# The second gate unit's multiply moved by two steps, and a new order in the tail, in a streaming-encoder block on one core

## The chip, the cores and the metric

The kernel runs on one core of one Trainium2 chip. The time is that of one execution on the device, in microseconds; a kernel's time is the median of its runs. A core has five engines with queues of their own: TensorE (PE), VectorE (DVE), ScalarE (ACT), GpSimd (POOL) and SyncE (SP). SP, ACT and POOL issue DMAs.

## What is computed

One layer over 512 tokens of 2048 features, all in float32, in this form:

```
h = rms_norm(x); q_a,k_a,v_a,q_g,k_g,v_g,r_g,gate_lr = split(h @ w_in)
y_a = chunked_band_attention(q_a, k_a, v_a)            # 16 heads of 64
o_g = rms_norm(gated_linear_attention(q_g, k_g, v_g))  # 4 heads of 256 values
y_g = o_g * silu(r_g)
x = x + concat(y_a, y_g) @ w_out
u = causal_conv3(rms_norm(x) @ w_ffn_up)               # 2 x 5632 columns
x = x + (gelu(u_gate) * u_val) @ w_ffn_down
x = x + sigmoid(rms_norm(x) @ w_ple_gate) * (p @ w_ple_proj)
return rms_norm(x)
```

## The kernel before

**Products.** Activations lie transposed, features on the 128 partitions and tokens along the free axis. A unit is one pair of 128-row blocks of a result (block m and block m + 8, or a gate and a value block). Each unit is computed by seven products in Strassen's manner, named P1 to P7, each over 256 tokens; a product is collected into a quarter of the unit's output tile `u` (C11, C12, C21, C22; the first digit is the block, the second the half of the tokens). Float32 precision comes from three passes with operands that are split into a high and a low half: high weights by high data, high weights by low data, low weights by high data. With 8 blocks of depth a product has 3 x 8 = 24 matmuls of 128 x 256. For each product ACT makes the high half of the weight page (`w<-s` or `w<-l`) and DVE the low half (`w<-s,w`); three page slots go round, so the high half of step i + 2 waits for the product of step i - 1. Some weight pages are sums of others: a load on SP and an adding DMA on POOL, or an addition on DVE (`s<-s,l`).

**Steps and agenda.** `steps` lists every product in order, and `agenda[i]` holds the pieces of side work of step i, each with a key. At step i the main loop runs the pieces with key 0, makes the high half for step i + 2, runs those with key 1, makes that page's low half, issues the product, runs the pieces with keys 2 to 8, and collects the product. PE, DVE and ACT execute in exactly this order (`in_order(True)`). The DMAs on SP and POOL are not held to it: a scheduler places them when the program is built.

**The front stage.** Its units are four of linear attention, eight of attention (`attend`) and four gate units (`after_gates`, u = 8 to 11, so g = 0 to 3), seven steps each. The second gate unit is g = 1: its products are steps 91 to 97, and its side work is counted from step 98, which is the first product of the third gate unit. That side work is: load `on` (the normed output of linear attention, from the DRAM tile `ond`) by SP; Silu of the unit's output on ACT; the multiply `u<-u,on` on DVE (`times`); and `pair`, which calls `store_pair`: three stores of `u` quarters, four differences on DVE into `tp`, and their four stores, all on SP. `after_gates` returns these pieces as tuples (steps later, key, function). For g = 2 the multiply and the pair come two steps later than the load. For g = 0 the whole list comes six steps after the unit's last product (`late`). After the front stage comes a stage of four steps for p @ w_ple_proj (`pp`), then `wo`, the product with w_out.

**The tail.** The last stage is the PLE gate. Its last two units, u6 and u7, end with the order P5, P5, P3, P3 written out by hand behind the main loop. `lo` is the first half of the tokens (0 to 255), `hi` the second. The helpers of the tail:

- `collect(u, "P3")`: DVE adds the product in PSUM to the unit's quarter (`u<-u,accC`).
- `times_norm(u, s, c)`: DVE multiplies a quarter by the norm's factor (`u<-u,rb`), then ACT takes the sigmoid.
- `add_gated(u, s, c)`: DVE multiplies by the embedding term and adds to the residual `xs`, ACT writes the square into `q`.
- `weigh_part`: ACT multiplies a block of `xs` by the final norm's weight.
- `sums_by_token`: PE sums squares over the partitions into `ms`. `root_begin` and `root_end`: ACT takes the square root, DVE refines it and writes two diagonals `dg`. `spread`: PE makes the row of factors `pb` from them.
- `finish(c, r, ms, queue)`: for each block pair m, DVE multiplies by `pb` and a DMA of 256 KB stores it, on SP or on the queue named. `turn` and `turned_out` do it another way for block pairs 0 to 3 of the second half: PE transposes, ACT evicts with the factor as a scale per partition, SP stores. `turn_first` and `turned_first_out` do that for block pair 4 of the first half.
- `act.activation(warm, ..., AF.Sqrt)` brings in the table of Sqrt ahead of its use.

Sixteen stores of 256 KB make the whole output: eight block pairs for each half of the tokens.

Of the kernel before, what the change touches and what calls it, by code (L numbers as in the profile page):

```python
# [11 lines left out]
AF = mybir.ActivationFunctionType  # L12
# [30 lines left out]
def encoder_block(ctx: ExitStack, tc: tile.TileContext, A, out):  # L43
    nc = tc.nc
# [25 lines left out]
    vec, act, ten = InOrder(nc.vector), InOrder(nc.scalar), InOrder(nc.tensor)  # L70
# [10 lines left out]
    ones = cp.tile([P, P], F32, name="ones")  # L81
# [3 lines left out]
    warm = cp.tile([P, 1], F32, name="warm")  # L85
# [3 lines left out]
    acc = cp.tile([P, T], F32, name="acc")  # L89
# [13 lines left out]
    def page(ring, name, dt=F32, shape=(P, 1024)):  # L103
        tags = rings[ring]
        i = counts.get(ring, 0)
        counts[ring] = i + 1
        tag = tags[i % len(tags)]
        return page_pool(tag).tile(list(shape), dt, tag=tag, name=name)
# [11 lines left out]
    def psum_aux(name):  # L120
        return aux[0](name)
# [106 lines left out]
    def xslot(i, name):  # L228
        return pairs[i % 8][:, i // 8, :]
# [7 lines left out]
    first = xslot(0, "x0_0")  # L237
# [307 lines left out]
    def bank(name):  # L545
        tag = banks.pop(0)
        return tag, pp_.tile([P, T], F32, tag=tag, name=name)
# [22 lines left out]
    def collect(unit, prod):  # L570

        if prod == "PP":
            return
        b = PRODUCTS[prod][2]
        tag, t = unit.banks[b]
        t = t[:, 0:256]
        unit.left[b] -= 1
        if unit.left[b] == 0:
            banks.append(tag)
        if unit.o is None:  # L580
            unit.o = page("u", "u").rearrange("p (s t) -> p s t", s=2)
        quarter, sign = {"P1": ("C11", 1), "P2": ("C11", 1), "P6": ("C12", 1), "P5": ("C22", -1),
                         "P7": ("C22", -1), "P3": ("C12", 1), "P4": ("C21", -1)}[prod]
        s, h = int(quarter[1]) - 1, int(quarter[2]) - 1
        dst = unit.o[:, s, 256 * h:256 * h + 256]
        if quarter not in unit.have:
            unit.have.add(quarter)
            act.activation(dst, t, AF.Copy, scale=float(sign))
        else:
            vec.tensor_tensor(dst, dst, t, ALU.add if sign > 0 else ALU.subtract)  # L590
        unit.parts[quarter] -= 1
        if unit.last is not None and unit.stage.quarter and unit.parts[quarter] == 0:
            unit.stage.quarter(unit, quarter)
# [282 lines left out]
    def after_gates(unit):  # L876
        g, M = unit.u - 8, {}

        def load():
            M["on"] = page("x" if g == 0 else "c", "on").rearrange("p (s t) -> p s t", s=2)  # L880
            nc.sync.dma_start(M["on"], ond[g])

        def times():
            vec.tensor_tensor(unit.o, unit.o, M["on"], ALU.mult)

        def pair():
            ops = store_pair(mixd if g < 2 else None, 4 + g, unit.o[:, 0, :], unit.o[:, 1, :])
            if g >= 2:
                tails[g - 2] = ops

        return [(0, 0, load), (0, 1, lambda: act.activation(unit.o, unit.o, AF.Silu)), (2 * (g == 2), 2, times), (2 * (g == 2), 3, pair)]

    def front_weights(u, q):
        j = ({"1": u, "2": 8 + u}[q[1]] if u < 8 else 24 + 2 * (u - 8) + (q[1] == "2") if u < 12 else
# [141 lines left out]
    def spare(name):  # L1036
        tag = free.pop(0)
        return page_pool(tag).tile([P, 1024], F32, tag=tag, name=name)

    def times_norm(unit, s, c):  # L1040
        o = unit.o[:, s, c]
        r = rb[:, None, c].broadcast_to([P, 2, 256]) if isinstance(s, slice) else rb[:, c]
        vec.tensor_tensor(o, o, r, ALU.mult)
        act.activation(o, o, AF.Sigmoid)

    def add_gated(unit, s, c):
        o, xs = unit.o[:, s, c], unit.xs[:, s, c]
        vec.tensor_tensor(o, o, unit.pp[:, s, c], ALU.mult)
        vec.tensor_tensor(xs, xs, o, ALU.add)
        if unit not in sq_page:  # L1050
            sq_page[unit] = spare("q").rearrange("p (s t) -> p s t", s=2)
        act.activation(sq_page[unit][:, s, c], xs, AF.Square)
# [524 lines left out]
    for i, (unit, prod) in enumerate(steps[:-4]):  # L1577
# [24 lines left out]
        if i - len(steps) in EARLY:  # L1602
            p, op, g = EARLY[i - len(steps)]
# [20 lines left out]
    def sums_by_token(parts, ms=None, done=True):  # L1624

        first = ms is None
        if first:
            ms = psum_aux("ms")[:, :2]
        for n, q in enumerate(parts):
            for t in range(2):  # L1630
                ten.matmul(ms[:, t:t + 1], q[:, t * P:t * P + P], ones[:, 0:1], start=first and n == t == 0,
                           stop=done and n == len(parts) - 1, skip_group_check=True)
        return ms

    def root_begin(ms):
        w = tp.tile([P, 4 * TT], F32, tag="tok", name="tok", bufs=2)
        a, y, t, r = (w[:, 2 * q:2 * q + 2] for q in range(4))
        act.activation(y, ms, AF.Sqrt, scale=1.0 / D, bias=epst)
        vec.tensor_scalar(a, ms, 1.0 / D, EPS, ALU.mult, ALU.add)
        return a, y, t, r  # L1640
# [11 lines left out]
    def spread(dg):  # L1652
        pb = bank("pb")[1][:, 0:256]
        ten.matmul(pb, ones, dg, start=True, stop=True)
        return pb

    def finish(c, r, ms, queue=None):
        for m in ms:
            t = x3[m][:, :, c]
            vec.tensor_tensor(t, t, r[:, None, :].broadcast_to([P, 2, 256]), ALU.mult)  # L1660
            (queue or nc.sync).dma_start(out2[m][:, :, c], t)

    u6, u7 = units[-2:]
    x3[6], x3[7] = u6.xs, u7.xs

    def weigh_part(unit, ss, c):
        for s in ss:
            m = unit.u + 8 * s
            act.activation(unit.xs[:, s, c], unit.xs[:, s, c], AF.Copy, scale=nfin[:, m:m + 1])


    def turn(n):
        t = bank("turned")[1]
        for b in range(4):
            m, s = 2 * (n % 2) + b // 2, b % 2
            c = slice(256 + n // 2 * P, 384 + n // 2 * P)
            ten.transpose(t[:, b * P:b * P + P], x3[m][:, s, c], ident)
        return t

    def turned_out(n, t, r):  # L1680
        if n % 2 == 0:
            turned_page[:] = [spare("turned")]
        o = turned_page[0][:, n % 2 * T:n % 2 * T + T]
        act.activation(o, t, AF.Copy, scale=r[:, n // 2:n // 2 + 1])
        m = 2 * (n % 2)
        nc.sync.dma_start(out2[m + n // 2][:, :, hi_half], o.rearrange("p (s t) -> p s t", s=2))
# [4 lines left out]
    def turn_first(m):  # L1691
        t = psum_aux("turned")
        for b in range(4):
            ten.transpose(t[:, b * P:b * P + P], x3[m][:, b % 2, b // 2 * P:b // 2 * P + P], ident)
        return t

    def turned_first_out(m, t, r):
        o = spare("turned")[:, :T]
        for i in range(2):
            c = slice(256 * i, 256 * i + 256)  # L1700
            act.activation(o[:, c], t[:, c], AF.Copy, scale=r[:, i:i + 1])
        nc.sync.dma_start(out2[m][:, :, lo_half], o.rearrange("p (s t) -> p s t", s=2))


    lo, hi = lo_half, hi_half
    sq = lambda u, s, c: sq_page[u][:, s, c]
    ms, rs = {}, {}
# [14 lines left out]
    w0 = root_begin(ms["lo"])  # L1722
# [6 lines left out]
    times_norm(u6, 0, hi)  # L1729
    weigh_part(u7, range(2), lo)  # L1730
    finish(lo, rs["lo"], (0,))
    add_gated(u6, 0, hi)
    weigh_part(u7, (1,), hi)
    weigh_part(u6, (1, 0), hi)
    finish(lo, rs["lo"], (1,))
    collect(u7, "P3")
    m1 = sums_by_token([acc[:, hi], sq(u6, 1, hi), sq(u7, 1, hi)], done=False)
    turned = [turn(n) for n in range(2)]
    m1 = sums_by_token([sq(u6, 0, hi)], m1, done=False)
    turned += [turn(n) for n in range(2, 4)]  # L1740
    first = turn_first(4)
    times_norm(u7, 0, hi)
    act.activation(warm, ones[:, 0:1], AF.Sqrt)
    finish(lo, rs["lo"], (2,))
    add_gated(u7, 0, hi)
    m1 = sums_by_token([sq(u7, 0, hi)], m1)
    finish(lo, rs["lo"], (3, 6))
    turned_first_out(4, first, w0[3])
    w1 = root_begin(m1)
    d1 = root_end(hi, *w1)  # L1750
    rs["hi"] = spread(d1)
    finish(lo, rs["lo"], (7,))
    turned_out(0, turned[0], w1[3])
    finish(hi, rs["hi"], (4,))
    turned_out(1, turned[1], w1[3])
    weigh_part(u7, (0,), hi)
    finish(hi, rs["hi"], (5,))
    turned_out(2, turned[2], w1[3])
    finish(hi, rs["hi"], (6,), nc.scalar)
    turned_out(3, turned[3], w1[3])  # L1760
    finish(hi, rs["hi"], (7,))
    finish(lo, rs["lo"], (5,), nc.scalar)


def _blocks(w):
# [73 lines left out]
```

## Time and profile before

| | |
|---|---|
| median of 3 runs | 2208.3 us (2207.74 to 2209.05) |
| profiled execution | 2206.61 us |
| its span on the core | 2204.7 us |
| granted TensorE clock, mean | 0.998 |
| PE busy | 2179.5 us (99%) |
| DVE busy | 1891.3 us (86%) |
| ACT busy | 1320.9 us (60%) |
| DMA traffic | 569.77 MB, mean 258 GB/s |

The span is the part of the execution in which the core's engines work; the profiled execution is 1.9 us longer. PE is busy for nearly all of the span, so the time moves where PE waits, at the start, at a few places within, and in the tail after its last product. All numbers of the trace come from this one execution, and times in it are counted from the start of the span. Lines are mostly given as L64, the helper through which ordered instructions pass, so instructions are told apart by engine and tiles, output first: `u<-u,on` reads tiles `u` and `on` and writes `u`.

### The profile page before, as it was taken

What the parts mean: (1) busy time and instruction counts of PE and PEld (TensorE: products, weight loads), DVE (VectorE), ACT (ScalarE), POOL (GpSimd) and SP (SyncE); (2) the same over time, 40 slices, a digit from 0 to 9 for tenths busy, and PEclk for the clock granted to TensorE, in tenths of its full rate; (3) what the DMA queues carried; (4) which work ended last, traced back from release to release, by engine and by line L of the source; (5) the groups of instructions that cost most, each with busy time, mean ns of one, the idle gap of its engine ahead of it and who ended that gap; (6) DMA issues with size and microseconds to landing.
All of it is one profiled execution on the core that took longest, in us unless ns stands there. A gap on an engine that the chain in (4) does not pass through costs nothing.

```text
span 2204.7 us, 45658 instructions
## 1 busy us (share of the span) xinstructions
PE 2179.5 (99%) x18248; PEld 2128.6 (97%) x18248; DVE 1891.3 (86%) x2601; ACT 1320.9 (60%) x1960; POOL 201.3 (9%) x245
## 2 busy tenths in 40 slices
PE   9999999999999999999999999999999999999997
PEld 7879999999899999999999999999999999999997
DVE  6876879998688889999888888889898797898997
ACT  6654567777575665555555555555564554666765
POOL 1021011111000001111111110000000100000000
PEclk9999999999999999999999999999999999999999
DMA  5498798898978989999999987887866967879896
GB/s 205 134 268 238 206 245 239 216 249 242 366 259 269 345 234 267 296 298 300 289 273 293 271 241 212 227 220 211 254 240 232 324 223 240 324 256 349 276 303 204
DMA packets 202341, 569.77 MB, mean 258 GB/s; under 512 B 22065, under 2 KB 64305, under 8 KB 202129
## 3 DMA queue, kind: packets, MB, share of 16 engines
q1 hardware_dynamic: 167792, 448.06, 57.3%
q0 software_dynamic: 32352, 115.88, 27.6%
q8 instruction: 143, 2.34, 0.4%
q10 hardware_dynamic: 1984, 2.92, 0.4%
q14 instruction: 70, 0.57, 0.1%
HBM read 493.37 MB, written 119.54 MB: 278 GB/s over the span
## 4 chain that ended last, share of the span: by engine, by line
PE 82%; DVE 8%; DMA 5%; ACT 2%; issue 2%; POOL 0%; DVEq 0%; SPq 0%; ACTq 0%; POOLq 0%
PE accA L64 41%; PE accC L64 20%; PE accB L64 10%; PE v L64 4%; DVE w L64 3%; PE vaA L64 2%; DVE h L64 1%; PE pp L64 1%; DVE u L64 1%; DMA on<-ond 1%; DMA s<-in_w_blk 1%; DMA s<-in_w_up 1%; DMA h<-h_T 1%; PE psc L64 1%; PE py L64 1%
## 5 line engine op out<-in xcount | busy, mean ns | idle before, releaser
L64 PE MATMUL accA<-h,w 128*128 128x256 f32 x5088 | 613.1, 277 | 2.5 <-ACT u L64 1.5
L64 PEld LDWEIGHTS accA<-h,w 128*128 128x128 f32 x5088 | 594.2, 188 | 5.6 <-ACT u L64 2.3
L64 DVE TENSOR_TENSOR w<-s,w 128x1024 fp32r<-128x1024 f32 (+1 forms) x381 | 457.5, 1201 | 68.4 <-ACT w L64 67.5
L64 PE MATMUL accC<-h,w 128*128 128x256 f32 x4248 | 509.9, 277 | 2.7 <-DVE w L64 2.7
L64 PEld LDWEIGHTS accC<-h,w 128*128 128x128 f32 x4248 | 494.4, 188 | 3.4 <-DVE w L64 3.1
L64 ACT ACTIVATE w<-l 128x1024 fp32r<-128x1024 f32 (+1 forms) x320 | 332.0, 1039 | 178.3 <-PE accC L64 116.9
L64 DVE TENSOR_TENSOR w<-l,w 128x1024 fp32r<-128x1024 f32 (+1 forms) x320 | 382.6, 1196 | 51.4 <-ACT w L64 49.2
L64 ACT ACTIVATE w<-s 128x1024 fp32r<-128x1024 f32 (+1 forms) x381 | 395.0, 1038 | 41.6 <-DVE s L64 28.7
L64 ACT ACTIVATE u<-accA 128x256 f32<-128x256 f32 x302 | 114.1, 378 | 349.0 <-PE accA L64 348.6
L64 DVE TENSOR_TENSOR s<-s,l 128x1024 f32<-128x1024 f32 (+1 forms) x176 | 211.3, 1201 | 18.1 <-DMA s<-in_w_blk 11.1
L64 POOL DMA_DIRECT2D s<-in_w_up x84 | 74.0, 881 | 716.3 <-DMA s<-in_w_up 335.8
L64 DVE SCALAR_TENSOR_TENSOR cv<-u,cw,cv 128x511 f32<-128x511 f32 (+1 forms) x176 | 131.6, 748 | 3.1
L64 PE MATMUL accA<-up_R,w 128*128 128x256 f32 x1056 | 127.0, 276 | 0.0
L64 PE MATMUL accA<-up_N,w 128*128 128x256 f32 x1056 | 126.7, 276 | 0.1
L64 PE MATMUL accB<-up_R,w 128*128 128x256 f32 x1056 | 126.7, 276 | 0.0
L64 PEld LDWEIGHTS accA<-up_R,w 128*128 128x128 f32 x1056 | 123.0, 188 | 0.5 <-issue 0.5
L64 PEld LDWEIGHTS accA<-up_N,w 128*128 128x128 f32 x1056 | 122.9, 188 | 0.3 <-ACT u L64 0.3
L64 PEld LDWEIGHTS accB<-up_R,w 128*128 128x128 f32 x1056 | 123.0, 188 | 0.0
L64 ACT ACTIVATE u<-accC 128x256 f32<-128x256 f32 x98 | 37.4, 381 | 91.0 <-PE accC L64 90.8
L64 PE MATMUL v<-w,h 128*128 128x512 f32 x384 | 88.7, 391 | 0.8 <-ACT h L171 0.8
L64 PEld LDWEIGHTS v<-w,h 128*128 128x128 f32 x384 | 71.9, 188 | 16.5 <-ACT h L171 1.0
L64 ACT ACTIVATE cv<-u,cw 128x512 f32<-128x512 f32 x88 | 67.1, 810 | 30.4 <-DVE u L64 30.4
(302 smaller groups left out, 2851.2 us busy)
## 6 DMA issues: line engine op xcount, KB each, us to landing
l<-in_w_up SPq DMA_DIRECT2D x132, 512.0 KB, 6.5
s<-in_w_up SPq DMA_DIRECT2D x84, 512.0 KB, 6.3
s<-in_w_up POOLq DMA_DIRECT2D x84, 512.0 KB, 7.9
l<-in_w_dn SPq DMA_DIRECT2D x56, 448.0 KB, 5.0
l<-in_w_blk SPq DMA_DIRECT2D x48, 512.0 KB, 5.2
s<-in_w_blk SPq DMA_DIRECT2D x32, 512.0 KB, 4.9
s<-in_w_blk POOLq DMA_DIRECT2D x32, 512.0 KB, 8.2
l<-in_w_out SPq DMA_DIRECT2D x28, 512.0 KB, 4.5
```

What stands on the lines that cost most here:

```text
L64: ins = f(*args, **kw)
```

## The change

It has two parts.

In `after_gates` the condition `g == 2` becomes `g in (1, 2)`: the second gate unit's `times` and `pair` run at step 100 in place of 98, with the same keys, behind the product of that step. Load and Silu stay at step 98.

In the tail, after the first output multiply of the first half, the order is written anew. The collection of u7's last product and its norm multiply come directly there. The three weightings of the second half that stood there go behind the beginning of the root. The sums of u6's last square come together with those of u7. All four transposed tiles and the fifth come in a row. The output multiplies of the first half are 1, 2, 3 ahead of the root and 6, 7, 5 behind it, where they were 1, 2, 3, 6 ahead, 7 behind and 5 at the very end. The turned block pair 4 is evicted behind the root's square root. The eviction of the last turned tile comes ahead of the store of block pair 6, and the store of block pair 7 of the second half goes to ACT's queue, which held that of block pair 5 of the first half. No instruction is added or dropped.

```
-        return [(0, 0, load), (0, 1, lambda: act.activation(unit.o, unit.o, AF.Silu)), (2 * (g == 2), 2, times), (2 * (g == 2), 3, pair)]
+        return [(0, 0, load), (0, 1, lambda: act.activation(unit.o, unit.o, AF.Silu)), (2 * (g in (1, 2)), 2, times), (2 * (g in (1, 2)), 3, pair)]
...
     finish(lo, rs["lo"], (0,))
+    collect(u7, "P3")
+    times_norm(u7, 0, hi)
     add_gated(u6, 0, hi)
+    act.activation(warm, ones[:, 0:1], AF.Sqrt)
+    m1 = sums_by_token([acc[:, hi], sq(u6, 1, hi), sq(u7, 1, hi)], done=False)
+    turned = [turn(n) for n in range(4)]
+    first = turn_first(4)
+    add_gated(u7, 0, hi)
+    m1 = sums_by_token([sq(u6, 0, hi), sq(u7, 0, hi)], m1)
+    finish(lo, rs["lo"], (1, 2, 3))
+    w1 = root_begin(m1)
+    turned_first_out(4, first, w0[3])
     weigh_part(u7, (1,), hi)
     weigh_part(u6, (1, 0), hi)
-    finish(lo, rs["lo"], (1,))
-    collect(u7, "P3")
-    m1 = sums_by_token([acc[:, hi], sq(u6, 1, hi), sq(u7, 1, hi)], done=False)
-    turned = [turn(n) for n in range(2)]
-    m1 = sums_by_token([sq(u6, 0, hi)], m1, done=False)
-    turned += [turn(n) for n in range(2, 4)]
-    first = turn_first(4)
-    times_norm(u7, 0, hi)
-    act.activation(warm, ones[:, 0:1], AF.Sqrt)
-    finish(lo, rs["lo"], (2,))
-    add_gated(u7, 0, hi)
-    m1 = sums_by_token([sq(u7, 0, hi)], m1)
-    finish(lo, rs["lo"], (3, 6))
-    turned_first_out(4, first, w0[3])
-    w1 = root_begin(m1)
     d1 = root_end(hi, *w1)
     rs["hi"] = spread(d1)
-    finish(lo, rs["lo"], (7,))
+    finish(lo, rs["lo"], (6, 7, 5))
     turned_out(0, turned[0], w1[3])
     finish(hi, rs["hi"], (4,))
     turned_out(1, turned[1], w1[3])
     weigh_part(u7, (0,), hi)
     finish(hi, rs["hi"], (5,))
     turned_out(2, turned[2], w1[3])
+    turned_out(3, turned[3], w1[3])
     finish(hi, rs["hi"], (6,), nc.scalar)
-    turned_out(3, turned[3], w1[3])
-    finish(hi, rs["hi"], (7,))
-    finish(lo, rs["lo"], (5,), nc.scalar)
+    finish(hi, rs["hi"], (7,), nc.scalar)
```

## The prediction, made before the run

> **What bounds the kernel now.** I began with the page, to see which engine holds the span.
>
> ```profile
> span 2204.7 us, 45658 instructions
> ...
> PE 2179.5 (99%) x18248; PEld 2128.6 (97%) x18248; DVE 1891.3 (86%) x2601; ACT 1320.9 (60%) x1960; POOL 201.3 (9%) x245
> ```
>
> TensorE (PE) is busy for all but about 25 us of the span, so a change can only win where PE stands idle, and only two such places touch this change. The first is around 550 us, at the end of the front stage. There I read the chain of waits, in order of time:
>
> ```profile
> 545.11 9.33 DMA on<-ond
> ...
> 554.53 1.24 DVE u L64
> ...
> 555.79 1.11 DVE tp L64 x3
> ...
> 557.26 1.23 DVE w L64
> ...
> 558.53 1.19 PE accC L64 x8
> ```
>
> Read it downwards. The load of the second gate unit's `on` runs for 9.33 us, from 545.11 to 554.44. Only then does VectorE (DVE) run that unit's multiply (`u`, 1.24 us), then its pair of differences (`tp`), and only then, at 557.26, the low half of a weight page (`w`), for which PE waits until 558.53. The waits of 535 to 600 us put lengths to it:
>
> ```profile
> DVE u L64 <- DMA on<-ond: 3.7, 1, 3.7
> ...
> PE accC L64 <- DVE w L64: 2.5, 1, 2.5
> ```
>
> DVE stands still for 3.7 us with everything queued behind the multiply, and 2.5 us of that reach PE. That is the whole price of the place; there is no other PE wait in this stretch.
>
> The second place is the tail, after PE's last product near 2187 us, where a chain over ScalarE (ACT), DVE and PE leads through the last root to the output multiplies and their stores. Its rows stand below, where they are priced.
>
> **Part one: the second gate unit's multiply, two steps back.** No instruction is added or removed. The multiply, the four differences of its pair, and the seven stores that the pair issues move from step 98 to step 100 (a step is one product of 24 matmuls). What DVE is now free to do first is seen in the timeline; columns are start, length, engine, operation, and in brackets the idle time before it:
>
> ```profile
> 549.12 1.05 ACT L64 ACTIVATE w<-s 128x1024 fp32r<-128x1024 f32 x1
> ...
> 549.58 1.22 DVE L64 TENSOR_TENSOR w<-s,w 128x1024 fp32r<-128x1024 f32 x1
> ...
> 550.65 1.06 ACT L64 ACTIVATE w<-s 128x1024 fp32r<-128x1024 f32 x1 [0.48 <-PE accB L64]
> ...
> 551.36 2.88 PE L64 MATMUL accA<-h,w 128*128 128x256 f32 x24
> ...
> 554.08 1.98 PE L64 MATMUL accC<-h,w 128*128 128x256 f32 x16
> ...
> 558.39 0.41 DVE L64 TENSOR_TENSOR u<-u,accB 128x256 f32<-128x256 f32 x1
> ...
> 558.72 1.22 DVE L64 TENSOR_TENSOR s<-s,l 128x1024 f32<-128x1024 f32 x1
> ...
> 560.04 1.07 ACT L64 ACTIVATE w<-s 128x1024 fp32r<-128x1024 f32 x1 [5.37 <-DVE s L64]
> ```
>
> PE's steps are 2.72 us apart (551.36 to 554.08). Step 101 is the product at 554.08: 16 matmuls ran with the high half, then PE stopped for the low half. That low half needs only the high half made by ACT at 549.12 (done 550.17), and DVE is through with the previous low half at 550.80 (549.58 + 1.22). So in the new order DVE does it at 550.8, done about 552.0; PE's third pass of step 101 wants it at 554.08 + 1.81 (two thirds of 2.72) = 555.9. The wait is gone with 3.9 us to spare. Then follow the collection of step 99 (0.41), the sum page `s` (1.22) and the low half of step 102, whose high half ACT has ready at 550.65 + 1.06 = 551.71: 552.0 + 0.4 + 1.2 + 1.2 gives 554.8. There the multiply now stands, and its data landed at 554.44, so by these rows it waits for nothing. Multiply and differences take until 557.26 − 554.53 = 2.7 us later, 557.5. Behind them is queued the low half of step 103, then done at 558.7. Step 103 starts at 554.08 + 2 × 2.72 = 559.5 and wants it at 561.3. ACT's high half for that step, which now waits 5.4 us for the sum page, comes earlier too. So the moved work is covered by DVE's own slack, and if the load landed later than 554.8, 2.6 us of further lateness (561.3 − 558.7) would still cost PE nothing.
>
> The gain is thus 2.5 us, unless something else is late next. The stores' absolute time hardly moves (the multiply runs at 554.8 against 554.53), so the queues of SP and POOL see them where they were. But PE comes 2.5 us earlier to what follows, while loads do not. The nearest margin is the third gate unit:
>
> ```profile
> 565.57 0.61 SPq L881 DMA_DIRECT2D on<-ond  x1
> ...
> 575.96 1.22 DVE L64 TENSOR_TENSOR u<-u,on 128x1024 f32<-128x1024 f32 x1
> ...
> 578.60 2.88 PE L64 MATMUL accA<-h,w 128*128 128x256 f32 x24
> ...
> 578.69 1.22 DVE L64 TENSOR_TENSOR w<-s,w 128x1024 fp32r<-128x1024 f32 x1
> ```
>
> Its load was issued on SP at 565.57, and the landing times of the four such loads are these:
>
> ```profile
> DMA to landing us min/median/max: 8.8/9.3/10.1
> ```
>
> It lands between 574.4 and 575.7. DVE came to its multiply at 575.96 without waiting; 2.5 us earlier it arrives at 573.5 and waits 0.9 to 2.2 us, if the load itself is issued no sooner. Behind that multiply stand the differences and a low half that ended at 579.91 (578.69 + 1.22) where PE's third pass wanted it at 578.60 + 1.81 = 580.41: 0.5 us of slack. So 0.4 to 1.7 us could come back as a new PE wait. Against that, SP reaches this load behind weight pages whose release is a low half on DVE, and those come earlier. I take 0.2 us of loss: part one is worth −2.3 us, with bounds of −2.5 and −0.8.
>
> **Part two: the tail.** Again nothing is added or removed; the order of one engine against another changes. The rows:
>
> ```profile
> 2186.85 0.68 DVE L64 TENSOR_TENSOR x<-x,pb 128x512 f32<-128x512 f32 x1
> ...
> 2187.29 0.89 ACT L64 ACTIVATE xs<-xs,cols 128x256 f32<-128x256 f32 x2
> ...
> 2188.68 1.29 ACT L64 ACTIVATE xs<-xs,cols 128x256 f32<-128x256 f32 x3
> ...
> 2188.84 0.41 DVE L64 TENSOR_TENSOR u<-u,accC 128x256 f32<-128x256 f32 x1
> ...
> 2189.29 0.42 DVE L64 TENSOR_TENSOR u<-u,rb 128x256 f32<-128x256 f32 x1
> ...
> 2189.56 1.51 PE L64 MATMUL turned<-ident,x 128*128 128x128 f32 x12
> ...
> 2190.30 1.28 ACT L64 ACT_TABLE_LOAD   x1
> ...
> 2191.70 0.40 ACT L64 ACTIVATE q<-xs 128x256 f32<-128x256 f32 x1
> ...
> 2192.01 0.82 ACT L64 ACTIVATE turned<-turned,tok 128x256 f32<-128x256 f32 x2
> ...
> 2192.16 0.61 PE L64 MATMUL ms<-ones,q 128*128 128x1 f32 x4 [1.09 <-ACT q L64]
> ...
> 2193.10 0.16 DVE L64 TENSOR_SCALAR tok<-ms 128x2 f32<-128x2 f32 x1 [0.70 <-ACT tok L64]
> ...
> 2193.95 1.26 ACT L64 ACTIVATE turned<-turned,tok 128x512 f32<-128x512 f32 x2 [0.89 <-DVE tok L64]
> ...
> 2194.49 0.70 PE L64 MATMUL pb<-dg,ones 128*128 128x256 f32 x2 [1.72 <-DVE dg L64]
> ...
> 2195.22 1.29 DVE L64 TENSOR_TENSOR x<-x,pb 128x512 f32<-128x512 f32 x2 [0.20 <-PE pb L64]
> ```
>
> The collection (`u<-u,accC`) now stands right behind the first output multiply, which starts at 2186.85. Two such multiplies take 1.29 us, so they go 0.61 apart, and the collection starts at about 2187.45 where it started at 2188.84. The norm multiply follows 0.45 later, at 2187.90. ACT is through with the two weightings of 2187.29 at 2188.18 and now has no three weightings (1.29 us) ahead of the last sigmoid: that runs at 2188.35. DVE then does unit 6's multiply and add, ACT its square, ending near 2189.56. Behind it comes the table load, at about 2189.58 where it was 2190.30: 0.72 earlier. Unit 7's add is done by 2189.95 and its square waits only for that table: it starts at 2190.98, not 2191.70. PE is no hindrance: from 2188.4 its 20 transposes at 0.126 (12 in 1.51) and one group of sums (0.5) end near 2191.4, when the square ends. So the last sums, and with them the root, come 0.7 us earlier: DVE's first root step at 2192.4 for 2193.10, the spread `pb` at 2193.8 for 2194.49.
>
> What the root no longer has in front of it, it has behind it. Blocks 6, 7 and 5 of the first half now stand between the root and the four blocks of the second half, seven multiplies where six stood: DVE is through with the root's own steps at 2192.4 + 1.35 (2193.10 to the end of the diagonals at about 2194.45) = 2193.75, and 7 × 0.61 = 4.3 makes the end 2198.05, only 0.25 before the old one (2195.22 and five multiplies at 0.61, 2198.3).
>
> The end is not set by DVE, though, but by the stores. The first store was issued at the start of the first row, and the first one after the root in the second:
>
> ```profile
> 2187.56 4.64 SPq L1661 DMA_DIRECT2D out<-x  x4
> ...
> 2194.66 0.37 SPq L1686 DMA_DIRECT2D out<-turned  x1
> ```
>
> The next two rows are the DMA engines' busy tenths and GB/s in 40 slices of 0.5 us, from 2186 to 2206:
>
> ```profile
> DMA  1000094292490499980899999999999999000000
> GB/s 33 0 0 0 14 340 170 80 346 98 166 342 16 178 342 363 383 307 0 274 350 346 330 338 334 338 319 373 387 379 385 383 379 326 2 0 0 0 16 0
> ```
>
> Data runs from the sixth number (2188.5, 0.95 after the first issue), stands still in slice 19 (a zero at 2195.0), and then runs without a break to about 2203.0: that is 2.62 MB, ten blocks of 256 KB, in 7.4 us, 0.74 us for each. From 2195.6 on the tail is bound by bandwidth, and its end is that start plus ten blocks. All 16 blocks need 11.84 us of the 14.5 (2188.5 to 2203.0), so 2.66 us were lost to gaps. For the new order the gaps are: block 0 done at 2189.25, the next multiply ends at 2190.6 and its data starts 0.95 later, at 2191.55 (gap 2.3); three blocks run to 2193.75; the turned block 4, now behind the root's square root on ACT, is ready at about 2193.15 (0.82 for its two evictions), data at 2194.1 (gap 0.35), to 2194.85; block 6, multiplied from 2193.75, has data at 2195.35 (gap 0.5). Then eleven blocks wait in turn: 2195.35 + 11 × 0.74 = 2203.5. ACT has the evictions of the second half ready in time: three weightings at 0.43 from 2193.15 bring it to 2194.45, and evictions at 0.63 feed faster than 0.74. So the tail ends 0.5 us later, although its root is earlier; I take +0.4. If the stores were no bound, the root's whole 0.7 us would be won (−0.7). If the root came no earlier, block 6 would have data at 2196.05 and the end would be 2204.2 (+1.2). Those are the ends.
>
> The Trainium skill, page ScalarE: Activation LUTs, section What ACT_TABLE_LOAD costs, says that a change of table holds ScalarE for about 2.66 us, a load of 1.28 and a drain of 1.38, which speaks against a tail whose last square waits on it. The rows here show a load of 1.28 at 2190.30 and the square at 2191.70, so this trace does not show the drain; with it, the sum would be what the third rival gives.
>
> **Sum.** −2.3 + 0.4 = −1.9 us. The profiled execution took 2206.61 us, 1.9 more than its span and 1.7 less than the median of the runs, 2208.3; I take the difference over to the median: 2206.4 us. That is 0.09%, and about 0.2% (4.4 us) is what a measurement of this kernel can tell from no change.
>
> **The rivals.** *The gain in front is given back.* The wait at 558.53 goes, but DVE's late multiplies at the third unit, or a load that PE now reaches too early, return all 2.3 us. For it: 0.5 us of slack at 578.69. Against it: PE is so short of idle time that no loads bind it elsewhere. The time is 2208.3 + 0.4 = 2208.7.
>
> *Slower: the stall moves to the third unit.* SP executes in order. If the seven stores keep their place ahead of the third unit's load and come later by the two steps (2 × 2.72 = 5.4 us), the load goes out at 571.0 and lands at 579.8 at the earliest. Its multiply then starts 579.8 − 573.5 = 6.3 us late, 0.5 us is slack, and PE loses 5.8 us: −2.5 + 5.8 + 0.4 = +3.7, 2212.0 us; with a landing of 10.1 us, 2213.3. It turns the whole positive from the point where the load goes out 1.7 us later than 565.57 (a loss of 2.1 us), and passes 0.2% only with the later landings. Against it: the data to be stored are ready when they were before.
>
> *The last table load holds ScalarE 1.38 us longer in the new place.* The last square then starts at 2192.36, 0.66 later than before, the root likewise, block 6 has data at about 2196.7, and eleven blocks end at 2204.85: the tail is +1.85, the whole −0.45, 2207.9 us. That is the rule of the skill's page named above; the rows show the square straight behind the load, so it gets little.
>
> *Faster by over 4.4 us.* Nothing priced here reaches it (−2.5 − 0.7 = −3.2). SP's order is not written by hand, so loads elsewhere can shift either way; this is all that stands for it.
>
> **How the numbers follow.** The forecast gets 66%, the gain given back 10%, the table 2%, the third unit 14%, of which 8 lie past 0.2%, and faster by over 4.4 us 8%. That makes 0.66 + 0.10 + 0.02 + 0.06 = 0.84 for no change, 0.08 for slower and 0.08 for faster. The priced bounds, −2.5 − 0.7 and −0.8 + 1.2, give 2205.1 to 2208.7; the runs of before lie up to 0.7 us off their median, so the range is 2204.4 to 2209.4.
>
> **What would show it.** Right in front: no PE wait for `w` near 556, and the second multiply right behind a low half at 554 to 555 with little or no wait for `on`. Wrong: a wait of DVE for `on` at the third unit over 1 us with PE waiting about 578, or a load of `on` issued well after 565. Right in the tail (times less the 2.3 us of part one): last square at 2191.0, spread at 2193.8, and DMA saturated from about 2195.4 with its last data near 2203.5. Wrong: slices of zero GB/s after that, or the last data before 2202.5, which would mean that the root and not the stores sets the end.

## The result and the profile after

| | before | after |
|---|---|---|
| median (21 runs each) | 2208.7 us (2205.93 to 2212.8) | 2205.94 us (2200.5 to 2209.56) |
| ratio, 95% interval | | 0.9985 (0.9978 to 0.9991) |
| profiled execution, span | 2206.61, 2204.7 us | 2206.01, 2204.2 us |

The change makes the kernel 0.15% faster: by the ratio −3.3 us, with an interval of −4.9 to −2.0 (the medians differ by 2.8 us). The forecast was 2206.4 us, a gain of 1.9. So the direction holds, and the interval excludes no change, but the forecast gain lies just outside it on the small side. The two profiled spans differ by only 0.5 us, and the page looks as it did:

```profile
span 2204.2 us, 45657 instructions
...
PE 2180.5 (99%) x18248; PEld 2129.6 (97%) x18248; DVE 1890.5 (86%) x2601; ACT 1321.9 (60%) x1960; POOL 201.0 (9%) x245
```

One pair of spans says little here. The stretch between the first product with w_out and the first sums of the second half in the tail, which the change doesn't touch, takes 1578.3 us in before, 1579.3 in after and between 1576.8 and 1582.2 in the runs below. So both places are read from rows of their own.

**The front.** The timeline of after (start, length, engine, operation; in brackets the idle time before it and what ended it):

```profile
549.95 2.35 DVE L64 TENSOR_TENSOR w<-s,w 128x1024 fp32r<-128x1024 f32 x2
...
553.30 2.88 PE L64 MATMUL accC<-h,w 128*128 128x256 f32 x24
...
554.83 1.22 DVE L64 TENSOR_TENSOR u<-u,on 128x1024 f32<-128x1024 f32 x1
...
556.02 2.88 PE L64 MATMUL accA<-h,w 128*128 128x256 f32 x24
```

Two low halves follow each other from 549.95, so step 101 (553.30) runs with all 24 matmuls in one row where before showed 16 and 8. The multiply stands at 554.83 with no bracket, and the next step starts 2.72 later (556.02). No PE wait is left there. Later the same timeline shows what came late next:

```profile
567.49 0.32 SPq L302 DMA_DIRECT2D mix_T<-tp  x1
...
569.16 0.42 SPq L881 DMA_DIRECT2D on<-ond  x1
...
573.75 1.23 DVE L64 TENSOR_TENSOR u<-u,on 128x1024 f32<-128x1024 f32 x1 [1.24 <-DMA on<-ond]
...
578.81 1.58 ACT L64 ACTIVATE wo_R<-wo_R 128x1024 fp32r<-128x1024 f32 x2 [2.22 <-DMA wo_R<-mix_R]
...
583.60 0.49 PE L64 MATMUL pp<-ps,w 128*128 128x512 f32 x1 [0.22 <-ACT ps L64]
...
584.86 15.44 PE L64 MATMUL pp<-ps,w 128*128 128x512 f32 x66 [0.77 <-DVE ps L64]
```

The third unit's load goes out at 569.16, not 565.57. DVE waits 1.24 us for it, and no PE wait follows. ACT waits 2.22 us for the first attention page of w_out (`wo_R`). The split of the embedding operand `ps` queues behind that on ACT and DVE, and PE waits 0.22 and 0.77 us for `ps` at the start of `pp`. Before had no wait there; its row of `pp` has no bracket:

```profile
586.75 22.14 PE L64 MATMUL pp<-ps,w 128*128 128x512 f32 x96
```

On SP the second unit's seven stores stand ahead of these loads as they did, but they go out later: from 559.13 to 567.49 (the row of `mix_T` above is the last), where before had 557.62 to 562.56.

To compare kernels I use the starts of three PE rows: steps 98 and 105 (`accA<-in_R`) and the first `accA<-wo_R`. Seven steps without a wait are 7 x 2.72 = 19.04 us. The kernels of the table are those of the experiments below.

| kernel | PE wait near 556 | 98 to 105 | 105 to first w_out | both |
|---|---|---|---|---|
| before | 2.47 | 21.80 | 41.01 | 62.81 |
| tail_only | 3.27 | 22.93 | 41.76 | 64.69 |
| before_again | 3.44 | 24.64 | 41.76 | 66.40 |
| half_stores_old | 3.69 | 25.76 | 41.76 | 67.52 |
| before_again2 | 4.31 | 26.44 | 41.01 | 67.45 |
| one_step | 0.95 | 20.29 | 41.01 | 61.30 |
| early_load | none | 19.04 | 44.77 | 63.81 |
| after | none | 19.04 | 42.53 | 61.57 |
| front_only | none | 19.04 | 41.90 | 60.94 |
| filled_tail | none | 19.04 | 43.07 | 62.11 |
| late_split | none | 19.04 | 42.06 | 61.10 |
| half_stores_new | none | 19.04 | 41.72 | 60.76 |
| early_embedding | none | 19.04 | 41.58 | 60.62 |

The first five have the old front: mean 65.77. Five with the new one (after, `front_only`, `filled_tail`, `late_split`, `half_stores_new`) have a mean of 61.30. By these single executions the front is worth about −4.5 us, not −2.3; the old ones alone differ by 4.7.

**The tail.** Timeline of after:

```profile
2186.05 0.50 PE L64 MATMUL ms<-ones,acc 128*128 128x1 f32 x4
...
2186.47 0.41 DVE L64 TENSOR_TENSOR u<-u,accC 128x256 f32<-128x256 f32 x1
...
2188.60 1.28 ACT L64 ACT_TABLE_LOAD   x1
...
2189.89 0.20 ACT L64 ACTIVATE warm<-ones 128x1 f32<-128x1 f32 x1
2190.00 0.40 ACT L64 ACTIVATE q<-xs 128x256 f32<-128x256 f32 x1
...
2192.78 1.22 PE L64 MATMUL pb<-dg,ones 128*128 128x256 f32 x2 [1.72 <-DVE dg L64]
...
2193.84 1.88 DVE L64 TENSOR_TENSOR x<-x,pb 128x512 f32<-128x512 f32 x3
...
2197.57 2.52 SPq L1686 DMA_DIRECT2D out<-turned  x2
```

and its DMA engines' busy tenths and GB/s in 40 slices of 0.5 us, from 2186 to 2206:

```profile
DMA  0009500009999594499999999999999980000000
GB/s 0 0 8 334 182 0 0 0 14 326 348 350 338 197 356 168 170 383 358 330 346 352 299 358 344 322 381 375 352 328 379 385 305 0 0 0 0 16 0 16
```

Call C the start of the first sums of the second half (`ms<-ones,acc`): 2187.03 before, 2186.05 here. The last square starts at C + 3.95, the spread at C + 6.73. Blocks 6, 7 and 5 follow it on DVE (2193.84). Data run without a break from 2194.5 (C + 8.45) to about 2202.45 (C + 16.4), and the span ends at C + 18.15, where before ended at C + 17.67. In this pair of executions the root is earlier and the end later, as forecast.

### The profile page after: what moved, and what is told of

Same layout as the page of the kernel before. It is cut to its first block, busy times and chain, and to the rows that moved or that the text cites. A ratio compares the mean times of both kernels' runs of the same rounds, so it can differ in the third digit from the quotient of the medians.

```text
span 2204.2 us, 45657 instructions
## 1 busy us (share of the span) xinstructions
PE 2180.5 (99%) x18248; PEld 2129.6 (97%) x18248; DVE 1890.5 (86%) x2601; ACT 1321.9 (60%) x1960; POOL 201.0 (9%) x245
## 4 chain that ended last, share of the span: by engine, by line
PE 79%; DVE 9%; DMA 6%; ACT 3%; issue 3%; POOL 0%; ACTq 0%; DVEq 0%; SPq 0%; POOLq 0%
PE accA L64 40%; PE accC L64 20%; PE accB L64 10%; PE v L64 4%; DVE w L64 3%; DMA s<-in_w_up 2%; DMA s<-in_w_blk 1%; DVE u L64 1%; DVE h L64 1%; ACT w L64 1%; PE vaA L64 1%; DVE s L64 1%; PE py L64 1%; DMA h<-h_T 1%; PE psc L64 1%
## 5 line engine op out<-in xcount | busy, mean ns | idle before, releaser
L64 PEld LDWEIGHTS v<-w,h 128*128 128x128 f32 x384 | 71.8, 188 | 16.5 <-ACT h L171 1.0
```

The costliest lines, as they stand in the source:

```text
L64: ins = f(*args, **kw)
```

## The experiments

**Each part alone.** `front_only` has the first part, `tail_only` the second:

```
-  (2 * (g == 2), 2, times), (2 * (g == 2), 3, pair)      # front_only, from before
+  (2 * (g in (1, 2)), 2, times), (2 * (g in (1, 2)), 3, pair)
-  (2 * (g in (1, 2)), 2, times), (2 * (g in (1, 2)), 3, pair)      # tail_only, from after
+  (2 * (g == 2), 2, times), (2 * (g == 2), 3, pair)
```

> Only the first part: the second gate unit's multiply and pair two steps later, the tail as before. Theory A (the load's late landing held DVE and through it PE; the tail is bound by its stores): the PE wait of 2.5 us near 556 us is gone, about 1 us comes back as a PE wait at the start of the embedding products because the loads behind the moved stores go out later; the time is 1.2 to 2.5 us below before. Rival B (the gain in front is given back whole by the first products with w_out, and what was measured comes from the tail): the time is that of before within 0.5 us. The tail's length, from PE's last product to the end of the span, is that of before, 17.7 us, under both.

> Only the second part: the tail's new order, the gate units as before. Theory A: the front keeps its PE wait of 2.5 us; the tail from PE's last product to the end of the span is 18.1 us against 17.7, so the time is 0.3 to 0.6 us above before. Rival B: the tail gives the measured gain, 2 to 3 us below before. Rival C (the root sets the end, not the stores): the tail is 17.0 us, 0.7 us below.

Measured: `front_only` 2204.95 us against 2209.97, ratio 0.9976 (0.9965 to 0.9986), so −5.3 us (−7.7 to −3.1). `tail_only` 2210.95 us, ratio 0.9999 (0.999 to 1.0009). The front alone gives the gain, and more than the 1.2 to 2.5 us that I expected; 0.9 us of it came back at the embedding (41.90 against 41.01), as expected. The tail alone can't be told from zero: its interval runs from −2.2 to +2.0 us, which all but rules out the 2 to 3 us of rival B but covers both theory A and the 0.7 us of rival C. Its profile has 18.22 us from C to the end, as theory A said, not 17. `tail_only` has the old front, and its PE wait was longer than before's:

```profile
557.86 1.21 PE L64 MATMUL accC<-h,w 128*128 128x256 f32 x8 [3.27 <-DVE w L64]
```

3.27 us, not 2.47. So the next question was how long this wait is in other executions.

**Before, unchanged, twice more.** `before_again` and `before_again2` are the kernel before, profiled anew.

> The kernel before, once more, to see how much the wait in front varies from execution to execution. Theory E (the wait's length hangs on when PE arrives and when the load lands, and a long one also lowers the granted clock): from the start of step 98 to that of step 105 it takes between 21.8 and 26 us, and over 24.5 only where the granted clock falls below 1 behind the wait; with the multiply moved it took 19.04 in every profile. Rival: the 21.8 us of the profile before are what it always takes, within 0.3, and the larger ones came from the changed tails' programs.

> The kernel before, a third time, with the same two theories as for the second: 21.8 to 26 us from step 98 to step 105, over 24.5 only with the granted clock below 1, or 21.8 us within 0.3.

Measured: 2207.82 us (span 2205.9) and 2208.01 us (span 2206.1), one execution each. PE waited 3.44 and 4.31 us, and steps 98 to 105 took 24.64 and 26.44 us. The rival (21.8 within 0.3) is out; 26.44 lies even above my bound of 26. The timeline of `before_again2`:

```profile
543.16 0.32 SPq L881 DMA_DIRECT2D on<-ond  x1
...
553.66 1.23 DVE L64 TENSOR_TENSOR u<-u,on 128x1024 f32<-128x1024 f32 x1 [5.20 <-DMA on<-ond]
...
557.66 2.07 PE L64 MATMUL accC<-h,w 128*128 128x256 f32 x8 [4.31 <-DVE w L64]
...
559.53 4.85 PE L64 MATMUL accA<-h,w 128*128 128x256 f32 x24
...
564.22 2.88 PE L64 MATMUL accC<-in_R,w 128*128 128x256 f32 x24
```

Its load of `on` was issued at 543.16 and the multiply started at 553.66. In the five old fronts this load lands 8.52, 9.31, 9.48, 9.74 and 10.35 us after the start of step 98 (in the order of the table), and PE's wait is 6.04 or 6.05 us less each time. So the wait follows the landing one for one. Both the issue (1.8 us before step 98 to 1.4 behind it) and the time to landing (7.9 to 11.5 us) vary.

Behind the wait the matmuls slow down: the 8 take 1.87 us (559.53 − 557.66) where 0.91 is a third of a step, and the next step takes 4.69 (564.22 − 559.53) instead of 2.72. That is 2.9 us more than at full speed. Its table by stretch shows what goes with it (length, then busy time and count of PE, PEld, DVE, ACT and POOL, then the granted clock, DMA share and GB/s):

```profile
558.50:560.50 2.00, 2.00 (x11) 2.00 (x11) 1.95 (x3) 1.33 (x3) 0.00 (x0) 0.50 0.81 153
560.50:565.00 4.50, 4.50 (x28) 4.50 (x28) 2.78 (x4) 2.00 (x2) 0.00 (x0) 0.65 1.03 293
```

The granted clock is 0.50 and 0.65 of full speed there. In `before_again` (3.44 us) the same two stretches have 0.54 and 0.83; in `tail_only` (3.27 us) and in before they have 1.00. The rows of `tail_only`:

```profile
558.50:560.50 2.00, 2.00 (x19) 2.00 (x19) 1.94 (x3) 1.13 (x2) 0.00 (x0) 1.00 0.92 182
560.50:565.00 4.50, 4.50 (x40) 4.50 (x40) 4.11 (x5) 3.15 (x4) 0.00 (x0) 1.00 1.02 296
```

The Trainium skill, page TensorE: Matmul & The Clock Gate, section Part 1: The HAM clock gate, says that the clock falls to half after at least one idle window of about 3.4 us. The traces agree only in part: in `before_again2` the clock fell 3.5 us into the pause, but in `half_stores_old` 2.2 us into a pause of 3.69, and in `before_again` when PE had been running again for 0.5 us. The last section comes back to this. So the old order cost the wait and, in three of five executions, about 2 to 3 us of slow matmuls beside it. The execution on which I predicted was the cheapest of the five.

**One step instead of two, and the data earlier.** `one_step` moves the multiply by one step; `early_load` keeps it in place and issues the second unit's load on ACT's queue, so that it needn't follow the first one on SP.

```
+  ((0, 1, 2, 0)[g], 2, times), ((0, 1, 2, 0)[g], 3, pair)      # one_step, from before
+  (nc.scalar if g == 1 else nc.sync).dma_start(M["on"], ond[g])      # early_load, from before
```

> The kernel before, with the second gate unit's multiply and pair one step later, not two. Theory A: DVE comes to the multiply about 2.4 us before its data and waits; the low half of step 102 is done near 560.3 us (by the clock of the profile before) where PE wants it at 558.6, so a PE wait of 1 to 2.5 us stays, one step further on, and the stretch from step 98 to the first product with w_out takes 62 to 63.5 us. Rival: one step is enough to have the low half of step 101 ahead of the multiply, the PE wait is gone and the stretch takes 61 to 62 us.

> The kernel before, with the second gate unit's load of its multiply's operand issued on ACT's queue, which puts it some 7 us sooner; multiply and pair stand at their old place. Theory A (the multiply's data are late, and what is queued behind it waits): the operand has landed when DVE comes to it, DVE's wait and PE's wait of 2.5 to 3.3 us near 556 us go without the multiply being moved; from the start of step 98 to the first product with w_out it takes 60.9 to 62 us, as with the multiply moved (61.6, 60.9, 62.1), against 62.8 and 64.7 in the two old fronts; the time is 2 to 4 us below before. Rival D (the 2.7 us of DVE work at that place hold PE, whatever the data): at least 1.5 us of the PE wait stay.

Measured: `one_step` 2206.62 us (one execution, span 2204.8), `early_load` 2208.73 us against 2209.66, ratio 0.9993 (0.9982 to 1.0005). The timeline of `one_step`:

```profile
553.08 1.23 DVE L64 TENSOR_TENSOR u<-u,on 128x1024 f32<-128x1024 f32 x1 [2.25 <-DMA on<-ond]
...
558.55 1.20 PE L64 MATMUL accA<-h,w 128*128 128x256 f32 x8 [0.95 <-DVE w L64]
```

DVE still waits 2.25 us for `on`, and 0.95 of it reaches PE, where the old order let through 3.4 in the mean of five. Nothing waits at the embedding (41.01), so the two stretches end as short as with two steps: 61.30 us, in the range of the rival, although the wait that theory A expected is there (I had put it at 1 to 2.5 us and the stretches at 62 to 63.5). One execution can't rank one step against two. `early_load`:

```profile
552.24 1.22 DVE L64 TENSOR_TENSOR u<-u,on 128x1024 f32<-128x1024 f32 x1
...
580.92 1.58 ACT L64 ACTIVATE wo_R<-wo_R 128x1024 fp32r<-128x1024 f32 x2 [2.82 <-DMA wo_R<-mix_R]
...
585.71 0.50 PE L64 MATMUL pp<-ps,w 128*128 128x512 f32 x1 [0.82 <-ACT ps L64]
```

The multiply at 552.24 has no bracket and the wait near 556 is gone without any step being moved: late data were the cause there, and rival D is out. But 3.8 us come back at the embedding (44.77 against 41.01), which I had not expected. ACT waits for `wo_R`, then PE for `ps` twice (0.82 and 0.76 us), and the clock falls:

```profile
586.00:589.00 3.00, 2.24 (x7) 1.65 (x7) 3.00 (x3) 1.82 (x2) 0.00 (x0) 0.76 1.05 417
589.00:592.00 3.00, 3.00 (x11) 2.36 (x10) 2.85 (x6) 1.19 (x2) 0.00 (x0) 0.67 1.03 416
```

`filled_tail` has nearly the same two waits (0.72 and 0.76) at a clock of 1.00 and takes 43.07; so about 1.7 us of the loss go with the clock. The time was not won: the interval includes 1, where that of `front_only` excludes it.

**What was given back.** In after, ACT's 2.22 us for `wo_R` stood ahead of the `ps` split. `late_split` makes that page's halves one step later; `early_embedding` leaves that in, loads the embedding operand four steps earlier, splits it one step earlier, and takes the tail of `filled_tail` (below):

```
-  ("R11", (1, 1), ((4, 9), (4, 9)), (8, 1))      # late_split, from after
+  ("R11", (1, 1), ((5, 9), (5, 9)), (8, 1))
-  agenda[i0 + 2].append(... embedding_load ...); agenda[i0 + 6].append(... embedding_split ...)
+  agenda[i0 - 2].append(... embedding_load ...); agenda[i0 + 5].append(... embedding_split ...)      # early_embedding
```

> The changed kernel, with the splitting of the first operand of the w_out products (wo_R, R11, both groups) one step later. Theory A' (part of the front's gain is given back because ACT, in order, waits 2.2 us for the load of that operand and so makes the embedding's halves late, for which PE waits 1.0 us): ACT's wait for wo_R and PE's wait at the embedding's first products go, PE reaches the first product with w_out about 1 us sooner, and the time falls by about 1 us against the changed kernel. Rival: the embedding's operand is late by its own load, PE waits there as before, nothing is won.

> The changed kernel with the filled tail, the splitting of the first w_out operand one step later, and the embedding's operand loaded four steps and split one step sooner. Theory A' (the front gives back 0.7 to 2.1 us at the embedding because ACT and DVE split its operand behind other work that is held up): PE no longer waits at the embedding's first products; from step 98 to the first product with w_out it takes 60.1 to 60.5 us against 60.9 to 62.1; the tail takes 17.5 us; the time is 1.5 to 2 us below that of the changed kernel. Rival: the operand's load lands too late for the earlier split, ACT waits for it and with it the weight halves behind; the stretch takes 61 us or more, and only the tail's 0.6 us is won.

Measured: `late_split` 2205.61 us, ratio 0.998 (0.9972 to 0.9989). Its timeline:

```profile
579.63 1.58 ACT L64 ACTIVATE wo_R<-wo_R 128x1024 fp32r<-128x1024 f32 x2 [0.35 <-DMA wo_R<-mix_R]
...
582.18 1.82 DVE L64 TENSOR_TENSOR wo_R<-wo_R 128x1024 fp32r<-128x1024 f32 x2
...
584.26 1.22 DVE L64 TENSOR_TENSOR ps<-pT,ps 128x1024 fp32r<-128x1024 f32 x1
...
585.53 22.02 PE L64 MATMUL pp<-ps,w 128*128 128x512 f32 x95 [0.77 <-DVE ps L64]
```

ACT's wait is 0.35 and PE's 0.22 for ACT's half of `ps` is gone, yet the 0.77 for DVE's half is as it was; the two stretches are 0.5 us shorter, not 1, and by time the kernel can't be told from after. The operand itself had landed near 575.8, long before its split, so its load (the rival) is not what holds PE. On DVE the half of `ps` stands right behind those of `wo_R`, which the edit moved as well; so this run shows that the split stands too late in its queue, but not how much the wait for `wo_R` had to do with it. `early_embedding`, 2203.1 us against 2209.12, ratio 0.9975 (0.9964 to 0.9985):

```profile
581.13 3.06 PE L64 MATMUL accA<-h,w 128*128 128x256 f32 x24 [0.22 <-DVE u L64]
...
584.04 16.24 PE L64 MATMUL pp<-ps,w 128*128 128x512 f32 x70
...
620.08 4.95 PE L64 MATMUL accA<-wo_N,w 128*128 128x256 f32 x40 [1.36 <-DVE wo_N L64]
```

`pp` now starts without a wait, and the two stretches take 60.62, the least of all (I had expected 60.1 to 60.5). What is left is a wait of 0.22 us at the third unit and, further on, one of 1.36 for `wo_N`. It is the fastest version by median, but its interval overlaps that of `front_only` and of after, so this is not shown to be a gain over either.

**The tail's end.** `half_stores_old` and `half_stores_new` are before and after with only the first of each pair's two blocks stored, so half of the output is left out:

```
-  (queue or nc.sync).dma_start(out2[m][:, :, c], t)
+  (queue or nc.sync).dma_start(out2[m][:, 0:1, c], t[:, 0:1])      # and both turned stores likewise
```

> The kernel before, which stores only the first of the two blocks of every pair in the tail: 16 stores of 128 KB, so half of the output is left out; all arithmetic stays. Theory A (stores bind the end of the tail): the tail from PE's last product to the end of the span falls from 17.7 to about 14.4 us, that is to the last output multiply and one store behind it. Rival C (the root and the multiplies behind it set the end): it stays over 17 us.

> The changed kernel with the same half of the stores left out. Theory A: the tail falls from 18.15 to about 14.0 us; with the stores out of the way the earlier root counts, and the new order is 0.3 to 0.5 us shorter than the old one with half its stores, where with whole stores it is 0.35 us longer. Rival C: it stays over 17 us, and the sign of the difference is the same as with whole stores.

Measured: 2208.59 and 2199.51 us, one execution each. From C to the end of the span it takes 15.22 us with the old order (2191.48 to 2206.7), 14.76 with the new (2182.94 to 2197.7). Both are far below 17, so rival C is out and the stores do bind; but they fell less than I expected (14.4 and 14.0). The new order is now 0.46 shorter, within the expected 0.3 to 0.5. PE rows of the old and then of the new:

```profile
2191.48 0.50 PE L64 MATMUL ms<-ones,acc 128*128 128x1 f32 x4
...
2199.02 1.22 PE L64 MATMUL pb<-dg,ones 128*128 128x256 f32 x2 [1.73 <-DVE dg L64]
```

```profile
2182.94 0.50 PE L64 MATMUL ms<-ones,acc 128*128 128x1 f32 x4
...
2189.73 0.70 PE L64 MATMUL pb<-dg,ones 128*128 128x256 f32 x2 [1.72 <-DVE dg L64]
```

The spread comes 7.54 after C in the old order and 6.79 in the new. So the root is 0.75 earlier, and with whole stores none of that reached the end.

`filled_tail` gives the stores more to do ahead of the root: block 1 goes between the two `add_gated`, and block 6 ahead of the root.

```
     first = turn_first(4)
+    finish(lo, rs["lo"], (1,))
     add_gated(u7, 0, hi)
...
-    finish(lo, rs["lo"], (1, 2, 3))
+    finish(lo, rs["lo"], (2, 3, 6))
...
-    finish(lo, rs["lo"], (6, 7, 5))
+    finish(lo, rs["lo"], (7, 5))
```

> The changed kernel, with the output multiply of block pair 1 of the first half moved up between the two residual additions and that of block pair 6 moved from behind the root to ahead of it. No piece of the root's chain waits for either. Theory A (stores bind the end, so gaps between stores cost time): the root comes when it came, within 0.1 us, but the store data starts sooner; by working the stores through at 0.74 us each the last data lands 0.8 us sooner and the tail shortens from 18.15 to about 17.4 us. Rival C (the root sets the end): the tail stays at 18.15 us, within 0.2.

Measured: 2205.87 us, ratio 0.9981 (0.9972 to 0.999), which by time can't be told from after. From C to the end it takes 17.51 us (2186.49 to 2204.0), and 17.40 in `early_embedding`, which has the same tail. The three profiles with the tail of the change take 18.03 to 18.22. So the gaps between the stores were worth about 0.7 us, as expected, although the last sums came no earlier (2190.98, C + 4.49, against C + 4.40). Rival C is out here too.

## Why the prediction was right

*The mechanism in front* was right row by row: the low half of step 101 ahead of the multiply, the multiply at 554.83 (forecast 554.8), no wait for `on`, no PE wait near 556. The margin held as well: in `late_split` the moved multiply waited 0.72 us for `on`, and PE did not.

*Its size was not.* The term of −2.3 us, with bounds of −2.5 and −0.8, measured about −4.5 by the table, and −5.3 (−7.7 to −3.1) in `front_only`. The step that failed is "2.5 us of that reach PE. That is the whole price of the place". The wait of 2.47 was right for the one execution shown (by the starts of the steps even that one lost 21.80 − 19.04 = 2.76), but it was the shortest of five, whose mean is 3.44. I took the load's landing at 554.44 as fixed. Even the spread of the four landings that I quoted (8.8 to 10.1 us) would have given a wait of 1.9 to 3.2 us only, and the longest was 4.31. The lowered clock was missing altogether: no row of that execution showed it, and PE counts as busy while it runs slowly, so "a change can only win where PE stands idle" leaves it out.

*The third unit.* I priced it from 0.5 us of slack. That was a misreading: the low half at 578.69 belongs to step 110, which starts at 581.32 and wants it at 581.32 + 1.81 = 583.13, so the slack was 3.2. The load did go out past the point that I named for the rival to turn the whole slower (3.6 us later against 1.7). It then landed in 4.6 us instead of 8.8 or more, DVE's wait of 1.24 was covered, and PE lost nothing. In the five new fronts of the table this load landed within 4.6 to 7.1 us, and PE lost nothing there in any of them. Why it lands sooner is not shown, and my prediction had no reason for it, so that part was luck. A right slack would have put this rival at less.

*The gain given back* came, but at another place: the embedding, where I had not looked. 41.0 to 41.8 us became 41.7 to 43.1, 0.8 us by the means (41.46 and 42.26). My loss of 0.2 was too small and its place wrong. "The stores' absolute time hardly moves" failed too: the last of the seven went out 4.9 us later, and with them the loads behind.

*The tail.* Times from C, forecast and measured: last square 3.95 and 3.95, spread 6.77 and 6.73, unbroken data from 8.3 and 8.45, their end 16.5 and 16.4. What binds the end is shown: with half the stores both tails are 2.5 and 3.4 us shorter than their means with whole ones, and `filled_tail` won 0.7 with a root no earlier. The sign of the term is not shown. From C to the end the three new tails (after, `tail_only`, `late_split`) have a mean of 18.13, six old ones 17.71: +0.42 for +0.4. But the old ones scatter from 16.60 to 18.35, and C itself can be late: in `one_step` (16.60) it comes 1.08 us behind DVE's first output multiply, elsewhere 0.09 to 0.19. Counted from that multiply, with which both orders begin, the means are 18.29 and 18.02, +0.27, and the old ones still scatter over 0.8. The table load cost its 1.28 us, and the next instruction on ACT began 0.01 us later (2188.60 + 1.28 = 2189.88, `warm` at 2189.89), so the table rival had no ground.

*The sum.* −4.5 + 0.4 = −4.1 us lies within the measured −4.9 to −2.0, and the forecast of −1.9 just outside. The time forecast, 2206.4, came within 0.5 us of the median partly by luck: its gain was 0.9 too small by the medians, and its base, 2208.3 from 3 runs, 0.4 lower than the 2208.7 of 21.

## What to carry to other kernels

A wait for a load in one profiled execution is one draw: take several executions before calling it the price; here the landings of similar loads in one profile gave too narrow a spread. A pause of TensorE can also cost more than its length: here pauses of 2.37 us and more were followed by half speed in four executions and not in two. And when a queue is reordered, look for the next place at which its later loads are awaited, not only at the nearest.

## What the runs showed of the hardware

The length of a pause doesn't decide alone whether the clock falls. In `one_step` a wait of only 2.37 us, shortly before the tail, was followed by half speed, where 2.47 us in before and 3.27 in `tail_only` cost none:

```profile
2168.81 7.33 PE L64 MATMUL accA<-h,w 128*128 128x256 f32 x48 [2.37 <-ACT u L64]
```

```profile
2170.00:2173.30 3.30, 3.30 (x18) 3.30 (x17) 3.30 (x4) 2.83 (x4) 0.00 (x0) 0.50 0.56 163
```

In `half_stores_old` the clock fell within the pause (554.91 to 558.60):

```profile
554.90:557.10 2.20, 0.01 (x1) 0.00 (x0) 2.13 (x5) 0.00 (x0) 0.72 (x1) 1.00 1.02 365
557.15:558.60 1.45, 0.00 (x0) 0.00 (x0) 1.45 (x3) 0.00 (x0) 0.12 (x1) 0.50 1.15 206
```

In the traces' clock records the half speed lasted 3.41 us in `before_again`, `early_load` and `one_step`, and 6.83, twice that, in `half_stores_old` and `before_again2`. In all 13 profiles every length between two changes of the clock is a multiple of 3.413 us; in `before_again`, for one, full speed had lasted 552.96 us before, 162 times 3.413. This fits a decision every 3.41 us, at times that the pause doesn't set. Laid on these intervals, the 3.27 us of `tail_only` are 1.77 in one and 1.50 in the next, and the 2.47 of before 1.20 and 1.28. The four long pauses that were followed by half speed put 2.22 us (`half_stores_old`), 2.29 (`one_step`), 2.94 (`before_again`) and 3.41 (`before_again2`) into one interval. How much idle time it takes stays open: up to 1.80 us in an interval left the clock at 1.00 before the tail, yet in `early_load` 1.57 us (0.82 and 0.76, with one matmul between them) were followed by half speed.

In `tail_only`, `half_stores_old` and `before_again` the steps from this place to the embedding take 2.83 us instead of 2.72 (rows of 2.99 instead of 2.88) while the clock reads 1.00; that is the 0.75 us in their 41.76. I have no cause for it.

Loads of the same size and form (`on`) landed between 4.6 (after) and 11.8 us (`early_load`) after their issue. The tile's view of after, then of `before_again2`:

```profile
DMA to landing us min/median/max: 4.6/8.2/10.0
```

```profile
DMA to landing us min/median/max: 8.3/9.4/10.4
```
